# Score products of two attention branches: contraction over 128 rows in place of 64 and 96, on one Trainium2 core

## The chip, the core and the metric

The kernel runs on one core of one Trainium2 chip. The metric is the device time of an execution in microseconds (us); lower is better. Three executions of the kernel before took 1120.05, 1120.86 and 1121.12 us. The engines are named as the profile names them: PE is TensorE (PEld its weight loads), DVE is VectorE, ACT is ScalarE, POOL is GpSimd, SP issues the DMAs.

## The reference

Two decoder layers over 512 tokens of width 1024, in float32. Each layer norms x, multiplies it by one wide input matrix, and feeds four branches; their gated outputs are projected, merged and projected again. Two of the branches compute scores from queries and keys:

```python
# branch A: indexer, top 128 keys of each query, softmax attention over them (4 heads of 64)
idx_logits = jnp.einsum('bqhd,bsd->bqhs', iqb, ik)            # 4 indexer heads of 32, one key of 32
score = jnp.einsum('bqh,bqhs->bqs', iwb * IDX_W_SCALE, relu(idx_logits))
logits = jnp.einsum('bqhd,bqkhd->bhqk', qb, k_sel) * scale
# branch C: stick-breaking attention (4 heads of 64)
z = jnp.einsum('bqhd,bshd->bhqs', qb, k) * scale
wts = jnp.where(strict, jnp.exp(log_sigmoid(z) + after), 0.0)  # after: sums of log(1 - beta) over later keys
```

## The kernel before, in words

Every float32 operand of a product is held as two float32r halves, an upper one (h: the value rounded by a copy on ACT, `half_h`) and a lower one (l: what the rounding left, a subtraction on DVE, `half_l`). A product of two such operands is three matmuls, hh + hl + lh (`mm3`, lines 269 to 271). A head has 64 channels, so half of the 128 partitions would be idle in a score product; the kernel before uses this to save a matmul.

- Branch C, `use_cq` (line 673): the upper half of a head's queries stands twice, on partitions 0 to 63 and 64 to 127 of `cq`; the lower half stands once, in `cql[c]`, where the two heads of a pair share a tile (one on each half of the partitions). `use_ck` (line 682) puts the upper half of the keys on one half of the partitions of `ck` and the lower on the other. In `zmm` (line 699) the first matmul of a key block (line 703) contracts over 128 rows and gives (kh + kl) qh; the second (line 704) contracts over the 64 rows `rs` alone and adds kh ql. The blocks of a head have 512, 384, 256 and 128 columns; the last two share a PSUM bank and are one call, `zmm(2)`.
- Branch A, `use_t1` (line 641): after the rotary step and four transposes (`qktr`) the queries of a tile are kept as upper half and, on the other half of the partitions, lower half (`qT`), the upper half of the keys twice (`kT`), the lower once (`kTl`). `attend` (line 873) computes, for a head and two tiles of queries, a matmul over 128 rows (line 951) and one over 64 (line 952) for each tile, `lg`, with 128 and 256 columns in the first four units of a layer and 384 and 512 in the last four.
- The indexer, `use_t2` (line 795): three pieces of 32 columns, (h, h, l) of the queries against (h, l, h) of the keys, are put beside each other in `ist`, transposed (`iqtr`, `iktr`, lines 822 and 824), and contracted over 96 rows in `select` (line 847, `sc`).

Weights come in chunks of up to [128, 1024] by DMA (`raw`), are split on ACT (`wh`, line 246) and DVE (`wl`, line 248), four steps ahead of their use at most. A step is one group of products on PE. The order on each engine is the order in which the code runs: jobs (generators) hand over at `HOP`, `PE` and `STEP`, and their instructions stand in the engines' queues among the splits of that step. So an instruction of `use_cq` on DVE stands ahead of the weight split that is queued after it. The first layer begins with the jobs of `use_t1` for all four tiles of tokens beside the steps of `cq` and `ck`; then comes `CV` (`tpairs`, the product `tp`, whose two chunks are split during the steps of `ck`).

```python
                    nc.tensor.matmul(o, ck[:, 2 * c + b, ks], cq[:, 2 * c + b, j * P:], start=True, stop=False)
                    nc.tensor.matmul(o, ck[rs, 2 * c + b, ks], cql[c][rs, j * P:], start=False, stop=True)
```

Of the kernel before, what the change touches and what calls it, by code (L numbers as in the profile page):

```python
# [50 lines left out]
# Weight chunks in the order of their use, each [128, 1024] or less.  "t": some tiles of 128 rows with all  # L51
# columns of a group (tokens on the partitions of the product); "c": all rows of 128 columns (columns on the
# partitions); "w": half of the columns of a branch's projection; "p": half of w_ple.
# [11 lines left out]
# groups that take two tiles of tokens through each half of the chunks  # L65
# [7 lines left out]
def chunk_plan():  # L73
    """(kind, elements of a partition, argument, first step, last step) of each chunk of each layer."""
# [50 lines left out]
def lay_weights(w_in, w_branch, w_out, w_ple, w_ple_gate):  # L125
    parts = []

    def rows_in(a):
        """[n * 128, c] to [128, n * c]."""
        return a.reshape(-1, P, a.shape[1]).transpose(1, 0, 2).reshape(P, -1)  # L130
# [22 lines left out]
# buffers of each kind, and how many steps ahead of its use a weight chunk is split  # L153
QB, TB, SB, RAWB, WB, LEAD = 10, 25, 24, 3, 6, 4
# steps from the end of their operands to the stick-breaking heads, the selection and the attention, and the
# rounds of the selection in a step of B, D, the gates and the merges
STICKD, SELECT0, ATTEND0, RATES = 3, 8, 5, (1, 2, 3, 2)
# the start: sums of squares, norm, transposes, evacuation of a tile of tokens, split of the next weight chunk
# and products (of a tile of tokens with a chunk)
# [5 lines left out]
def split_steps(chunks):  # L165
    """The step in which each chunk is split in halves, and whether after the step's products."""
# [14 lines left out]
def hybrid_kernel(ctx: ExitStack, tc: tile.TileContext, w, x, p_t, pos, inv_freq, rows, small, ws_t, b_sp, out):  # L181
# [18 lines left out]
    def halves_cm(name):  # L200
        """Two split tiles of channels: (h, l), each [128, 2, 512]."""
        q = Q(name)
        return q[:, 0:2], q[:, 2:4]

    def halves_tm(name):
        """256 split columns of each tile of tokens: (h, l), each [128, 4, 256]."""
        q = Q(name).rearrange("p (a k) (b f) -> p a (k b) f", a=2, b=2)
        return q[:, 0], q[:, 1]

    def stacked(name):  # L210
        """256 columns of each tile of tokens, each head's 64 as their halves: [128, 4, 4, (h, l), 64]."""
        return Q(name).rearrange("p t (n a f) -> p t n a f", n=4, a=2)
# [38 lines left out]
    def due(late):  # L251
        """The splits of this step."""
# [13 lines left out]
    def mm3(ps, a, b, start, stop):  # L266
        """ps += a.T b of two split operands."""
# [25 lines left out]
    # A job yields HOP where another engine goes on, PE before products that wait for what it has just told,  # L293
    # and STEP behind them.
# [3 lines left out]
    def rounds(live):  # L298
        """Goes round the jobs until each of them has ended or waits; those that wait for products."""
# [47 lines left out]
    def row(l, o, name):  # L347
        """1024 of rows, on every partition."""
# [31 lines left out]
    # key blocks of a unit, with the column at which each starts  # L380
# [37 lines left out]
    def make_masks():  # L418
# [4 lines left out]
        # -1 where row >= column  # L423
# [4 lines left out]
        # far below where the key (row) is not before the query (column)  # L428
# [6 lines left out]
    def rstd(v, parts, n):  # L435
        """v = (sum(parts) / n + eps) ** -0.5 of columns."""
# [8 lines left out]
    def rstd2(v, ss):  # L445
        """The same of two halves of which the first is divided and has eps."""
# [4 lines left out]
    def turn_blocks(name, src):  # L451
        """The four [128, 128] blocks of src, each transposed."""
# [23 lines left out]
    def weigh(out, v, j, n, wh, wl, start, stop):  # L476
        """The keys of block j by their weights: the halves of the values' products, one above the other."""
# [13 lines left out]
    def tgroup(lhs, cols, use, apart=None, finish=None):  # L491
        """Token-major products: use(t, psum) is the job that goes on with a tile of tokens.  With apart,
        two tiles at a time, the second job that many steps behind the first.  With finish, the
        last tile goes by halves of the columns: finish(t, psum, columns) is their job."""
# [24 lines left out]
    def tpairs(lhs, use):  # L519
        """The same for 256 columns, two tiles at a time."""  # L520
# [11 lines left out]
    def ccol(use):  # L532
        """Channel-major products of the normed input: use(psum) is the job that goes on."""
        k, = take()
        ps = bank("cc")
        step(lambda: cmm(ps, k))
        front.append(use(ps))
# [45 lines left out]
    # the first group of products takes tokens and weights as they come in  # L583
# [27 lines left out]
    for l in range(L):  # L611
# [12 lines left out]
        kT = Q("kT")  # L624
        kTl = halves_cm("kTl")[0]
# [15 lines left out]
        def use_t1(t, ps):  # L641
# [5 lines left out]
            # queries: the upper half and, on the other half of the partitions, the lower; keys: the upper  # L647
            # half twice, and the lower
# [3 lines left out]
            k = kT.rearrange("p (c b) s -> p c b s", c=2)  # L652
# [5 lines left out]
            for b in range(2):  # L658
                half_l(q[ROWS[b], :, b], q[ROWS[1 - b], :, b], pv[ROWS[b], 0:2], QK_SCALE)
                half_l(k[ROWS[b], :, b, sl], kTl[ROWS[b], :, sl], pv[ROWS[b], 2:4])  # L660
# [8 lines left out]
        chained[0] = False  # L669
        cq, ck = Q("cq"), Q("ck")  # L670
        cql = [T(f"cql{c}", dt=F32R) for c in range(2)]

        def use_cq(c, ps):
            """Queries of two heads: the upper half twice (on both halves of the partitions), and the lower."""
# [4 lines left out]
            for b in range(2):  # L679
                half_l(cq[ROWS[b], 2 * c + b], cql[c][ROWS[b]], ps[ROWS[b]], QK_SCALE)  # L680

        def use_ck(c, ps):
            """Keys of two heads: the upper half and, on the other half of the partitions, the lower."""
# [11 lines left out]
        def stick(c, b):  # L695
# [3 lines left out]
            def zmm(u):  # L699
                ps = bank("cz")  # L700
                for j, c0 in UNITS[u]:
                    o, ks = ps[:, c0:c0 + S - j * P], slice(j * P, (j + 1) * P)
                    nc.tensor.matmul(o, ck[:, 2 * c + b, ks], cq[:, 2 * c + b, j * P:], start=True, stop=False)
                    nc.tensor.matmul(o, ck[rs, 2 * c + b, ks], cql[c][rs, j * P:], start=False, stop=True)
                return ps

            def smm(u):
                """Sums over the keys behind each key, without those of the later blocks in common()."""
# [5 lines left out]
            def sums(ps, first, blocks, own=None):  # L714
                """Sums of blocks of keys; of their own, over the later keys."""
# [6 lines left out]
            def common():  # L722
                """What the two last blocks of keys add to both of the first."""
# [71 lines left out]
        def use_t2(t, ps):  # L795
# [8 lines left out]
            # query halves (h, h, l) against key halves (h, l, h), stacked along the contraction  # L804
            st = T("ist", (P, 5, 3, 32), F32R)
            rq = r[:, :128].rearrange("p (h f) -> p h f", h=4)
            rk = r[:, 128:160]
            if t:
                A.copy(st[:, 0:4, 0], rq)
                A.copy(st[:, 0:4, 1], rq)  # L810
            A.copy(st[:, 4, 0], rk)
            A.copy(st[:, 4, 2], rk)
            yield HOP
            if t:
                V.tensor_tensor(st[:, 0:4, 2], rq, st[:, 0:4, 0].bitcast(F32), op=ALU.subtract)
            V.tensor_tensor(st[:, 4, 1], rk, st[:, 4, 0].bitcast(F32), op=ALU.subtract)
            yield PE
            sf = st.rearrange("p h c f -> p h (c f)").bitcast(F32)
            if t:
                tp = bank("iqtr")  # L820
                for h in range(4):
                    nc.tensor.transpose(tp[:96, h * P:(h + 1) * P], sf[:, h], ident)
            tk = bank("iktr")
            nc.tensor.transpose(tk[:96, :P], sf[:, 4], ident)
            yield STEP
            if t:
                q = T("iqT", dt=F32R)
                A.copy(q[:96], tp[:96])
                iqT[t] = q
            V.tensor_copy(ikT[:96, t * P:(t + 1) * P], tk[:96, :P])  # L830
# [5 lines left out]
        def select():  # L836
            """bias[i]: 0 at the keys that each query of tile i keeps, far below at the others."""
# [460 lines left out]
```

## Time and profile before

| what | value |
|---|---|
| executions | 1120.05, 1120.86, 1121.12 us (median 1120.86) |
| span of the profiled execution | 1118.6 us, first to last instruction |
| median less span | 2.3 us, what lies around the span |
| PE busy | 1109.1 us (99%), 5300 matmuls |
| DVE busy | 760.5 us (68%) |
| ACT busy | 492.6 us (44%) |
| POOL busy | 23.7 us (2%) |
| chain that ended last | PE 95% |
| granted TensorE clock | mean 1.000 |

The profile's busy time of PE counts overlapped, pipelined matmuls, so 99% does not say that PE works at its peak; the distance between the starts of two matmuls that follow each other does. In a timeline row the columns are start (us), duration (us), engine, line, operation, output and inputs, shape (rows of contraction * columns of the stationary operand, then the moving operand), count, and, in brackets, idle time of the engine before it with what ended it.

### The profile page before, as it was taken

How to read it: one execution, taken by the hardware profiler on the slowest of the kernel's cores; microseconds unless marked ns; L12 is line 12 of the kernel's file. 1: busy time of each engine (PE TensorE's matmuls, PEld its weight loads, DVE VectorE, ACT ScalarE, POOL GpSimd, SP SyncE). 2: the span in 40 equal slices, each digit the busy share in tenths (PEclk: the TensorE clock that was granted, in tenths of full speed). 3: DMA queues.
4: the chain of work that ended last, by engine and by line, in shares of the span. 5: the costliest groups of instructions: out<-in, count | busy, mean ns of one | idle time of the engine just before them, and what ended most of it. 6: DMA issues, size and time to landing. Idle time of an engine off the chain costs nothing.

```text
span 1118.6 us, 13984 instructions
## 1 busy us (share of the span) xinstructions
PE 1109.1 (99%) x5300; PEld 924.3 (83%) x5300; DVE 760.5 (68%) x1420; ACT 492.6 (44%) x857; POOL 23.7 (2%) x46
## 2 busy tenths in 40 slices
PE   8999999999999999999999999999999999999998
PEld 6888888888888888888788988988888888888887
DVE  5967769866788754547577677698668886454562
ACT  5566654323423433434446576433243244333341
POOL 2000000000000000000000000000000000000000
PEclk9999999999999999999999999999999999999999
DMA  5232232322233223542522222313222322226331
GB/s 193 84 109 76 76 99 58 113 76 76 76 94 94 76 90 99 170 151 95 166 97 81 78 74 76 100 61 111 82 86 71 99 76 76 95 94 205 114 114 38
DMA packets 34349, 109.01 MB, mean 97 GB/s; under 512 B 4057, under 2 KB 4841, under 8 KB 34282
## 3 DMA queue, kind: packets, MB, share of 16 engines
q1 hardware_dynamic: 34218, 108.10, 30.2%
q8 instruction: 41, 0.67, 0.2%
q0 software_dynamic: 64, 0.03, 0.1%
q14 instruction: 26, 0.21, 0.1%
HBM read 103.91 MB, written 4.19 MB: 97 GB/s over the span
## 4 chain that ended last, share of the span: by engine, by line
PE 95%; ACT 1%; DVE 1%; DMA 1%; issue 1%; SPq 0%; POOL 0%; DVEq 0%; ACTq 0%
PE mg L269 11%; PE mg L270 10%; PE mg L271 10%; PE tg L269 7%; PE tg L271 7%; PE tg L270 7%; PE cc L269 6%; PE cc L271 6%; PE cc L270 6%; PE z L270 3%; PE z L271 3%; PE z L269 3%; PE tp L270 1%; PE tp L269 1%; PE cs L719 1%; PE tp L271 1%
## 5 line engine op out<-in xcount | busy, mean ns | idle before, releaser
L248 DVE TENSOR_TENSOR wl<-raw,wh 128x1024 fp32r<-128x1024 f32 (+1 forms) x180 | 217.2, 1211 | 19.6 <-ACT wh L246 18.8
L269 PE MATMUL mg<-hh,wh 128*128 128x512 f32 x512 | 201.0, 392 | 0.0
L270 PE MATMUL mg<-hl,wh 128*128 128x512 f32 x512 | 199.4, 389 | 0.0
L271 PE MATMUL mg<-hh,wl 128*128 128x512 f32 x512 | 199.3, 389 | 0.0
L246 ACT CAST wh<-raw 128x1024 fp32r<-128x1024 f32 (+1 forms) x180 | 185.4, 1038 | 10.6 <-DMA raw<-in_w 4.1
L1085 ACT ACTIVATE g<-mg,prm 128x512 f32<-128x512 f32 x64 | 44.2, 690 | 231.0 <-PE mg L271 231.0
L269 PE MATMUL cc<-hh,wh 128*128 128x512 f32 x320 | 126.0, 394 | 0.0
L271 PE MATMUL cc<-hh,wl 128*128 128x512 f32 x320 | 124.8, 390 | 0.0
L270 PE MATMUL cc<-hl,wh 128*128 128x512 f32 x320 | 124.7, 390 | 0.0
L269 PEld LDWEIGHTS mg<-hh,wh 128*128 128x128 f32 x512 | 96.1, 188 | 21.9 <-issue 1.5
L271 PEld LDWEIGHTS mg<-hh,wl 128*128 128x128 f32 x512 | 96.1, 188 | 20.1
L270 PEld LDWEIGHTS mg<-hl,wh 128*128 128x128 f32 x512 | 96.1, 188 | 19.4
L1091 DVE SCALAR_TENSOR_TENSOR g<-g,z 128x512 f32<-128x512 f32 x48 | 32.9, 686 | 72.7 <-PE z L271 72.6
L271 PEld LDWEIGHTS cc<-hh,wl 128*128 128x128 f32 x320 | 60.1, 188 | 12.8
L269 PEld LDWEIGHTS cc<-hh,wh 128*128 128x128 f32 x320 | 60.1, 188 | 12.3 <-issue 0.7
L270 PEld LDWEIGHTS cc<-hl,wh 128*128 128x128 f32 x320 | 60.2, 188 | 11.6
L865 DVE MAX8 m<-cur 128x8 f32<-128x256 f32 (+2 forms) x96 | 53.6, 559 | 4.4 <-POOL cur L857 2.6
L866 DVE MATCH_REPLACE8 cur<-m,cur 128x256 f32<-128x256 f32 (+2 forms) x96 | 52.1, 543 | 0.0
L269 PE MATMUL tg<-wh,xh 128*128 128x512 f32 (+1 forms) x136 | 51.7, 380 | 0.0
L271 PE MATMUL tg<-wh,xl 128*128 128x512 f32 (+1 forms) x136 | 51.3, 377 | 0.0
L270 PE MATMUL tg<-wl,xh 128*128 128x512 f32 (+1 forms) x136 | 51.3, 377 | 0.0
L269 PE MATMUL tg<-wh,mh 128*128 128x512 f32 x128 | 50.0, 390 | 0.0
(251 smaller groups left out, 2019.5 us busy)
## 6 DMA issues: line engine op xcount, KB each, us to landing
raw<-in_w SPq DMA_DIRECT2D x172, 512.0 KB, 3.5
raw<-in_w SPq DMA_DIRECT2D x8, 420.0 KB, 3.1
x<-in_x SPq DMA_DIRECT2D x8, 256.0 KB, 5.6
res<-in_x SPq DMA_DIRECT2D x8, 256.0 KB, 4.3
xdram<-res SPq DMA_DIRECT2D x8, 256.0 KB, 3.5
res<-xdram SPq DMA_DIRECT2D x8, 256.0 KB, 5.6
out<-res SPq DMA_DIRECT2D x7, 256.0 KB, 2.1
gpost<-in_rows SPq DMA_DIRECT2D x2, 512.0 KB, 5.7
```

The costliest lines, as they stand in the source:

```text
L246: A.copy(h[:, :n], r[:, :n])
L248: V.tensor_tensor(lo[:, :n], r[:, :n], h[:, :n].bitcast(F32), op=ALU.subtract)
L269: nc.tensor.matmul(ps, ah, bh, start=start, stop=False)
L270: nc.tensor.matmul(ps, ah, bl, start=False, stop=False)
L271: nc.tensor.matmul(ps, al, bh, start=False, stop=stop)
L719: nc.tensor.matmul(ps[:, (i - first) * P:], tri if i == own else ones, sh[u][q][:, ci:ci + S - i * P], start=(i == blocks[0] and q == 0), ...
L865: V.max(m8, cur[:, :n])
L866: V.match_replace(cur[:, :n], m8, cur[:, :n], TAKEN)
L1085: A.activation(g, ps, AF.Tanh, bias=b_merge(n, dt), scale=0.5)
L1091: V.scalar_tensor_tensor(g, g, 1.0, z, op0=ALU.add, op1=ALU.mult)
```

## The change

All score products contract over 128 rows.

- `kTl` becomes a tile of the shape of `kT`: the lower half of the keys stands on both halves of the partitions. `use_t1` writes it twice (a second subtraction for each b). Line 952 multiplies all 128 rows of `qT` (upper and lower half) by it: kl (qh + ql).
- `cql` becomes four tiles, one for each head, with the lower half of the queries on both halves of the partitions; `use_cq` writes each twice. Line 704 multiplies all 128 rows of `ck`: (kh + kl) ql.
- The indexer stacks four pieces of 32, (h, h, l, l) against (h, l, h, l), in two tiles `isq` and `isk` of their own in place of `ist`; transposes, copies and products take 128 rows.

```diff
-        kTl = halves_cm("kTl")[0]
+        kTl = Q("kTl")
...
-                half_l(k[ROWS[b], :, b, sl], kTl[ROWS[b], :, sl], pv[ROWS[b], 2:4])
+                for o in (ROWS[b], ROWS[1 - b]):
+                    half_l(k[o, :, b, sl], kl[o, :, b, sl], pv[ROWS[b], 2:4])
...
-        cql = [T(f"cql{c}", dt=F32R) for c in range(2)]
+        cql = [T(f"cql{h}", dt=F32R) for h in range(4)]
...
-                half_l(cq[ROWS[b], 2 * c + b], cql[c][ROWS[b]], ps[ROWS[b]], QK_SCALE)
+                for o in (ROWS[b], ROWS[1 - b]):
+                    half_l(cq[o, 2 * c + b], cql[2 * c + b][o], ps[ROWS[b]], QK_SCALE)
...
-                    nc.tensor.matmul(o, ck[rs, 2 * c + b, ks], cql[c][rs, j * P:], start=False, stop=True)
+                    nc.tensor.matmul(o, ck[:, 2 * c + b, ks], cql[2 * c + b][:, j * P:], start=False, stop=True)
...
-            st = T("ist", (P, 5, 3, 32), F32R)
-            rq = r[:, :128].rearrange("p (h f) -> p h f", h=4)
+            sk = T("isk")[:, :P].rearrange("p (a b f) -> p a b f", a=2, b=2)
             rk = r[:, 128:160]
+            rk2 = rk[:, None, :].to_broadcast([P, 2, 32])
             if t:
-                A.copy(st[:, 0:4, 0], rq)
-                A.copy(st[:, 0:4, 1], rq)
-            A.copy(st[:, 4, 0], rk)
-            A.copy(st[:, 4, 2], rk)
+                sq = T("isq", (P, 4, 2, 2, 32))
+                rq = r[:, :128].rearrange("p (h f) -> p h f", h=4)
+                for a in range(2):
+                    A.copy(sq[:, :, 0, a].bitcast(F32R), rq)
+            for a in range(2):
+                A.copy(sk[:, a, 0].bitcast(F32R), rk)
             yield HOP
             if t:
-                V.tensor_tensor(st[:, 0:4, 2], rq, st[:, 0:4, 0].bitcast(F32), op=ALU.subtract)
-            V.tensor_tensor(st[:, 4, 1], rk, st[:, 4, 0].bitcast(F32), op=ALU.subtract)
+                for a in range(2):
+                    V.tensor_tensor(sq[:, :, 1, a], rq, sq[:, :, 0, a], op=ALU.subtract)
+            V.tensor_tensor(sk[:, :, 1], rk2, sk[:, :, 0], op=ALU.subtract)
...
-                            nc.tensor.matmul(ps[k][:, :n], iqT[i][:96, (h + k) * P:(h + k + 1) * P], ikT[:96, :n], start=True, stop=True)
+                            nc.tensor.matmul(ps[k][:, :n], iqT[i][:, (h + k) * P:(h + k + 1) * P], ikT[:, :n], start=True, stop=True)
...
-                        nc.tensor.matmul(ps[:, :w], qT[t][rs, c, n % 2], kTl[rs, c, :w], start=False, stop=True)
+                        nc.tensor.matmul(ps[:, :w], qT[t][:, c, n % 2], kTl[:, n, :w], start=False, stop=True)
```

The number and the order of the instructions on PE, ACT, POOL and SP stay as they are. On DVE, 30 instructions are added. The first place is DVE's queue in the first layer, from the last job of `use_t1` to the splits of the two chunks of `CV` (the `wl` rows). Before:

```order
L285 SCALAR_TENSOR_TENSOR qT<-qktr,qT 64x2x128
L283 TENSOR_TENSOR kTl<-qktr,kT 64x2x128
L285 SCALAR_TENSOR_TENSOR cql_438<-cc,cq 64x512 x2
L248 TENSOR_TENSOR wl_593<-raw_431,wh_592 128x1024
L283 TENSOR_TENSOR ck<-cc,ck 64x512 x2
L248 TENSOR_TENSOR wl_636<-raw_456,wh_635 128x1024
```

And in the change:

```order
L285 SCALAR_TENSOR_TENSOR qT<-qktr,qT 64x2x128
L283 TENSOR_TENSOR kTl<-qktr,kT 64x2x128 x2
L285 SCALAR_TENSOR_TENSOR cql_439<-cc,cq 64x512 x2
L285 SCALAR_TENSOR_TENSOR cql_440<-cc,cq 64x512 x2
L248 TENSOR_TENSOR wl_601<-raw_431,wh_600 128x1024
L283 TENSOR_TENSOR ck<-cc,ck 64x512 x2
L248 TENSOR_TENSOR wl_650<-raw_458,wh_649 128x1024
```

A second `kTl` subtraction stands behind each first one (eight in a layer), and two more of `cql` behind each pair (four in a layer); the splits `wl` come after them, in the same order as before.

The second place is DVE's queue during the stick-breaking heads of the first layer, at a tile of the indexer. Before:

```order
L248 TENSOR_TENSOR wl_1007<-raw_827,wh_1006 128x1024
L815 TENSOR_TENSOR ist<-ir,ist 128x4x32
L816 TENSOR_TENSOR ist<-ir,ist 128x32
L283 TENSOR_TENSOR cwl<-cz,cwh 128x384
L740 SCALAR_TENSOR_TENSOR csp<-cz,csp 128x384
```

And in the change (whose lines stand two to five further down):

```order
L248 TENSOR_TENSOR wl_1021<-raw_841,wh_1020 128x1024
L820 TENSOR_TENSOR isq<-ir,isq 128x4x32 x2
L821 TENSOR_TENSOR isk<-ir,isk 128x2x32
L283 TENSOR_TENSOR cwl<-cz,cwh 128x384
L742 SCALAR_TENSOR_TENSOR csp<-cz,csp 128x384
```

One subtraction more stands ahead of the stick-breaking head's `cwl`, for three of the four tiles of a layer.

## Rows read from the trace of the kernel before

**Rows 1.** The page, busy time and share of each engine.
```profile
PE 1109.1 (99%) x5300; PEld 924.3 (83%) x5300; DVE 760.5 (68%) x1420; ACT 492.6 (44%) x857; POOL 23.7 (2%) x46
```
**Rows 2.** Groups of PE by shape: line, count | busy us, mean ns | idle before.
```profile
L704 PE MATMUL cz<-cql,ck 64*128 64x384 f32 x8 | 3.5, 439 | 0.0
L847 PE MATMUL sc<-ikT,iqT 96*128 96x384 f32 x8 | 2.1, 338 | 0.0
L480 PE MATMUL cav<-cwl,vc 128*128 128x384 f32 x8 | 2.7, 335 | 0.0
```
**Rows 3.** Timeline of PE, 131.0 to 133.0 us, branch C in the first layer.
```profile
131.09 0.28 PE L703 MATMUL cz<-cq,ck 128*128 128x256 f32 x1
131.30 0.38 PE L704 MATMUL cz<-cql,ck 64*128 64x256 f32 x1
131.61 0.33 PE L703 MATMUL cz<-cq,ck 128*128 128x128 f32 x1
131.87 0.32 PE L704 MATMUL cz<-cql,ck 64*128 64x128 f32 x1
132.12 0.39 PE L479 MATMUL cav<-cwh,vc 128*128 128x256 f32 x1
132.35 0.28 PE L480 MATMUL cav<-cwl,vc 128*128 128x256 f32 x1
132.47 0.22 PE L479 MATMUL cav<-cwh,vc 128*128 128x128 f32 x1
132.53 0.28 PE L480 MATMUL cav<-cwl,vc 128*128 128x128 f32 x1
132.64 0.44 PE L719 MATMUL cs<-sph,tri 128*128 128x512 f32 x1
132.92 0.39 PE L719 MATMUL cs<-spl,tri 128*128 128x512 f32 x1
```
**Rows 4.** Timeline of PE, 382.4 to 384.6 us, a late unit of the attention.
```profile
382.45 0.42 PE L951 MATMUL lg<-kT,qT 128*128 128x384 f32 x1
382.81 0.44 PE L952 MATMUL lg<-kTl,qT 64*128 64x384 f32 x1
383.18 0.50 PE L951 MATMUL lg<-kT,qT 128*128 128x512 f32 x1
383.61 0.50 PE L952 MATMUL lg<-kTl,qT 64*128 64x512 f32 x1
384.04 0.50 PE L269 MATMUL mg<-hh,wh 128*128 128x512 f32 x1
384.38 0.39 PE L270 MATMUL mg<-hl,wh 128*128 128x512 f32 x1
```
**Rows 5.** Groups by shape, DVE: the lower half of the keys.
```profile
L283 DVE TENSOR_TENSOR kTl<-qktr,kT 64x256 fp32r<-64x256 f32 x16 | 6.8, 422 | 0.2
```
**Rows 6.** Timeline of DVE, 55 to 64 us, first layer.
```profile
55.99 0.42 DVE L285 SCALAR_TENSOR_TENSOR qT<-qktr,qT 64x256 fp32r<-64x256 f32 x1 [0.34 <-ACT kT L277]
...
58.42 1.39 DVE L285 SCALAR_TENSOR_TENSOR cql<-cc,cq 64x512 fp32r<-64x512 f32 x2 [0.70 <-ACT cq L279]
59.84 1.23 DVE L248 TENSOR_TENSOR wl<-raw,wh 128x1024 fp32r<-128x1024 f32 x1
...
62.52 1.23 DVE L248 TENSOR_TENSOR wl<-raw,wh 128x1024 fp32r<-128x1024 f32 x1
```
**Rows 7.** Timeline of PE, 61 to 66 us, first step of `CV`.
```profile
63.80 0.39 PE L270 MATMUL tp<-wl,hh 128*128 128x256 f32 x1 [0.27 <-DVE wl L248]
```
**Rows 8.** Timeline of DVE, 607 to 610 us, second layer: the same split.
```profile
608.42 1.22 DVE L248 TENSOR_TENSOR wl<-raw,wh 128x1024 fp32r<-128x1024 f32 x1
```
**Rows 9.** Timeline of PE, 614 to 615.2 us: the matmul that needs that split.
```profile
614.75 0.28 PE L270 MATMUL tp<-wl,hh 128*128 128x256 f32 x1
```
**Rows 10.** Waits: engine and line, waited for, total us, times, longest us.
```profile
DVE pr L902 <- PE lg L952: 37.2, 28, 3.5
...
DVE qT L285 <- ACT kT L277: 7.1, 4, 5.1
```

More of the change, by code (lines that the diff above doesn't have):

```diff
@@ L651, in use_t1 @@
             sl = slice(t * P, (t + 1) * P)
-            k = kT.rearrange("p (c b) s -> p c b s", c=2)
+            k, kl = kT.rearrange("p (c b) s -> p c b s", c=2), kTl.rearrange("p (c b) s -> p c b s", c=2)
             for b in range(2):
@@ L803, in use_t2 @@
             half_l(va[:, t, :, 0], va[:, t, :, 1], heads(ps[:, 0:256]))
-            st = T("ist", (P, 5, 3, 32), F32R)
-            rq = r[:, :128].rearrange("p (h f) -> p h f", h=4)
+            sk = T("isk")[:, :P].rearrange("p (a b f) -> p a b f", a=2, b=2)
             rk = r[:, 128:160]
+            rk2 = rk[:, None, :].to_broadcast([P, 2, 32])
             if t:
-                A.copy(st[:, 0:4, 0], rq)
-                A.copy(st[:, 0:4, 1], rq)
-            A.copy(st[:, 4, 0], rk)
-            A.copy(st[:, 4, 2], rk)
+                sq = T("isq", (P, 4, 2, 2, 32))
[4 more added lines that the diff above has]
+                A.copy(sk[:, a, 0].bitcast(F32R), rk)
             yield HOP
             if t:
-                V.tensor_tensor(st[:, 0:4, 2], rq, st[:, 0:4, 0].bitcast(F32), op=ALU.subtract)
-            V.tensor_tensor(st[:, 4, 1], rk, st[:, 4, 0].bitcast(F32), op=ALU.subtract)
+                for a in range(2):
+                    V.tensor_tensor(sq[:, :, 1, a], rq, sq[:, :, 0, a], op=ALU.subtract)
+            V.tensor_tensor(sk[:, :, 1], rk2, sk[:, :, 0], op=ALU.subtract)
             yield PE
-            sf = st.rearrange("p h c f -> p h (c f)").bitcast(F32)
             if t:
@@ L821, in use_t2 @@
                 for h in range(4):
-                    nc.tensor.transpose(tp[:96, h * P:(h + 1) * P], sf[:, h], ident)
+                    nc.tensor.transpose(tp[:, h * P:(h + 1) * P], sq[:, h].rearrange("p a b f -> p (a b f)"), ident)
             tk = bank("iktr")
-            nc.tensor.transpose(tk[:96, :P], sf[:, 4], ident)
+            nc.tensor.transpose(tk[:, :P], sk.rearrange("p a b f -> p (a b f)"), ident)
             yield STEP
@@ L827, in use_t2 @@
                 q = T("iqT", dt=F32R)
-                A.copy(q[:96], tp[:96])
+                A.copy(q, tp)
                 iqT[t] = q
-            V.tensor_copy(ikT[:96, t * P:(t + 1) * P], tk[:96, :P])
+            V.tensor_copy(ikT[:, t * P:(t + 1) * P], tk[:, :P])
         tgroup(hlhs, 420, use_t2, 1)
@@ L944, in attend @@
                     m2, n = units[k]
-                    c, rs = n // 2, slice(64 * (n % 2), 64 * (n % 2) + 64)
+                    c = n // 2
                     lg[k] = []
```

## The prediction

> **What bounds the kernel now.** I read the busy times first, then the groups by shape, then the timelines of PE and DVE around the edited lines, then the waits. PE is busy for 99% of the span [rows 1] and has almost nothing to wait for, so an edit pays only if the matmuls themselves follow each other faster, and costs only where it makes PE wait. Whether they follow fast is read from the distance between two starts. In the stick-breaking head at 131 us [rows 3] the reader finds both patterns side by side, with the same widths. Matmuls over 128 rows: 256 columns take 0.12 us from start to start (132.35 to 132.47), 128 columns 0.06 and 0.11, 512 columns 0.23 or, right behind a 128-column one, 0.28. With the 64-row matmul of line 704 between them: the 256-column matmul of line 703 ahead takes 0.21, the 64-row one 0.31, and the first one behind the block (132.12) still 0.23 where 0.12 is normal. So a 64-row matmul alone costs 0.09 + 0.19 + 0.11 = 0.39 us more than a 128-row one: 0.09 ahead of it, 0.19 itself, 0.11 behind. The attention shows the same [rows 4].
>
> Is it the number of rows? The groups by shape say so: at 384 columns a 64-row matmul lasts 439 ns, the indexer's 96-row one 338, a 128-row one 335 [rows 2]. So 96 rows cost nothing extra, and 64 do.
>
> **What the change removes.** There are 64 such matmuls: in each layer 16 of line 704 and 16 of line 952.
> - The call `zmm(2)` has two of them, with 256 and 128 columns, 8 calls in all. From 131.09 to the second start behind it, 132.35, it takes 1.26 us [rows 3]. At 128 rows the same five distances are 0.12 + 0.12 + 0.06 + 0.11 + 0.17 (0.12, and 0.05 more behind a 128-column matmul) = 0.58. Gain 0.68, times 8: 5.4 us.
> - The calls with 384 and with 512 columns have one each, 16 in all: 0.39 each, 6.2 us.
> - The first four units of the attention in a layer have two, with 128 and 256 columns, 8 in all. I take the 0.68 of `zmm(2)`, less 0.03 because these stand behind 128-column transposes, which make a start late in either kernel: 0.65, 5.2 us.
> - The last four units have 384 and 512 columns, 8 in all. From 382.45 to 384.38 is 1.93 us [rows 4]; at 128 rows 0.18 + 0.18 + 3 x 0.23 = 1.05, and I leave 0.08 for the transposes ahead: gain 0.8, 6.4 us.
>
> Sum: 5.4 + 6.2 + 5.2 + 6.4 = 23.2 us. The indexer's products and transposes go from 96 to 128 rows or columns and gain nothing [rows 2].
>
> The rows say that a 64-row matmul is dearer than a 128-row one, 439 against 335 ns [rows 2]. The Trainium skill, "TensorE: Matmul & The Clock Gate", section "Why this matters for your kernels", states the contrary: one matmul over 32 rows takes as long as one over 128, and few rows pay only where several run at once. By that rule the 23.2 us would be 0 and only the additions below would be left, 1126.3 us (rival 4); the rows contradict it for this kernel, and I go by them.
>
> The gain stays if DVE and ACT keep up with a PE that reaches each point earlier. In the attention they do: DVE waits for the scores in 28 places, 37.2 us in all [rows 10], more than the 11.6 us that the attention saves; with the scores earlier, it starts earlier. In the stick-breaking heads no row shows PE waiting.
>
> **What it adds.** All of it is on DVE.
> - First layer. DVE gets 8 more subtractions of `kTl` and 4 more of `cql` ahead of the splits of `CV`. A `kTl` one lasts 422 ns [rows 5], 0.43 from start to start; two of `cql` take from 58.42 to 59.84 [rows 6], 0.71 each. That is 8 x 0.43 + 4 x 0.71 = 6.2 us. DVE has no room there: the only idle times are 0.34 and 0.70 us, both waits for ACT that the later DVE would no longer see [rows 6], so 5.2 us remain. And the stretch already ends on PE's path: the second split of `CV` runs from 62.52 to 63.75 [rows 6], and the matmul that needs it starts at 63.80, after PE stood idle for it [rows 7]. Nothing covers the shift. This matmul should start at 63.8 + 5.2 = 69.0: **5.2 us lost**, in two waits, a long one at the first split of the group and about 1.2 us at the second. What is queued behind on DVE (keys of `ck`, the split of the next group) is late as well, but its users on PE come later by the same amount.
> - Second layer. The same additions, but the split ends at 608.42 + 1.22 = 609.64 [rows 8] and is needed at 614.75 [rows 9], 5.1 us of cover. The idle times before `qT` come to 7.1 us in four places; 5.1 of it is the wait before the first, 0.3 belongs to the first layer [rows 6, 10], so 1.7 absorb part of the 6.2. A delay of 4.5 us stays under 5.1: cost nothing. Were the cover gone, each us of further delay would be a us of PE.
> - Indexer. Six more subtractions of half the width of a `kTl` one, so at most 6 x 0.42 = 2.5 us if PE waited for all of them; at least 0. PE waits for nothing near them, so I am near the lower end: 0.2 us. Copies of 128 partitions for 96 keep their columns; I take 0.
>
> The upper and lower end of the additions are 7.7 us (6.2, plus 2.5, less the idle 1.0) and, should the second copies cost less than the first or the wait at `CV` be overrated, 0.
>
> **Sum.** The profiled execution spans 1118.6 us; the median of the runs is 1120.9, 2.3 more, and I take these 2.3 as lying outside the span. 1120.9 - 23.2 + 5.2 + 0.2 = **1103.1 us**.
>
> **Rivals.**
> 1. *The stall at `CV` does not come, or is far shorter*: 1120.9 - 23.2 + 0.2 = 1097.9. For it: the idle times of DVE there are few but the shift is a sum of twelve small prices. Against it: PE already waits at exactly this split [rows 7].
> 2. *The stall puts TensorE's clock down.* The mean granted clock before is 1.000, the upper level of 2.4 GHz, with PE busy for 99% of the span [rows 1]. After a stall of about 4 us it could be granted 1.2 GHz for a time. The step of `CV` where this happens has 48 matmuls of 0.12 us [rows 3], 5.8 us; at half the clock all of it would cost 5.8 more, none of it 0. Half: 3 us, 1106. The Trainium skill, "TensorE: Matmul & The Clock Gate", section "Why this matters for your kernels", warns of idle gaps between bursts for this reason; no row of this trace shows a fall.
> 3. *The heads' chains on DVE and ACT become the bound.* PE issues each head's products up to 0.7 us earlier per step, while additions, exponentials and splits between two products take as long as ever. If half of the 11.6 us of the stick-breaking heads is lost in waits for `spl` and `cwl`: 1109. Against it: no such wait shows now; for it: the trace shows no spare time directly either.
> 4. *The number of rows costs nothing, and the change does not do what it is built for* (the other side). Place: the same 64 matmuls. The distances would come from something that stays, such as two matmuls with different moving tiles into one bank. Then the gain is 0 and the stall remains: 1120.9 + 5.4 = 1126.3. It decides as soon as less than 5.4 of the 23.2 us is won, that is, if a second matmul over 128 rows still costs 0.30 of its 0.39 us. Against it: lines 479 and 480 also accumulate two matmuls with different tiles into one bank, at 0.12 and 0.06 [rows 3].
>
> **Chances.** My forecast 0.60; rival 1 0.12; rival 2 0.13; rival 3 0.09; rival 4 0.06. The range 1097.5 to 1108 holds the forecast with its unknown prices and rivals 1 and 2, and leaves out rivals 3 and 4, 0.15. A difference of 0.2% (2.2 us) is about what a measurement can tell from none. All but rival 4 are faster by more; 0.01 of that one I count as no change: faster 0.94, same 0.01, slower 0.05.
>
> **What the profile of the changed kernel would show.** Start-to-start distances of 0.12 and 0.06 us in `zmm(2)`, and groups of lines for the second score product at the same mean as line 480's. PE waiting for `wl` at the `CV` group of the first layer, some 4 us and then 1 us, with DVE without idle time from 47 us to there; no such wait in the second layer. The granted clock at 1.000; below that, rival 2. New waits of PE for `spl`, `cwl` or `isq` would speak for rival 3; distances of 0.3 us at 128 rows for rival 4. The forecast is wrong if the time is above 1108 or below 1097.5, and its working is wrong if the two terms, 23.2 won and 5.2 lost, don't show apart.

## The result, and the profile after

The change takes the kernel from 1120.95 us (median of 4 executions, 1120.05 to 1121.12) to **1103.86 us** (4 executions, 1102.33 to 1104.97): ratio 0.985, 95% interval 0.984 to 0.986. The profiled execution is the one of 1104.97 us; its span is 1103.3.

The busy times of the page after the change, to be read against [rows 1]: PE has 20.6 us less, DVE 11.3 us and 30 instructions more.

```profile
PE 1088.5 (99%) x5300; PEld 923.3 (84%) x5300; DVE 771.8 (70%) x1450; ACT 492.3 (45%) x857; POOL 23.0 (2%) x46
```

Groups of PE by shape after the change, with 384 columns: the second score products of both branches and the indexer's, now all of 128 rows. The 439 ns of [rows 2] are gone; the indexer's 338 ns have become 335.

```profile
L706 PE MATMUL cz<-cql,ck 128*128 128x384 f32 x8 | 2.7, 337 | 0.0
...
L956 PE MATMUL lg<-kTl,qT 128*128 128x384 f32 x8 | 2.7, 335 | 0.0
...
L851 PE MATMUL sc<-ikT,iqT 128*128 128x384 f32 x8 | 2.0, 335 | 0.0
```

Timeline of PE after the change, the same `zmm(2)` as in [rows 3]. From the first start to the second start behind the block it takes 134.97 - 134.39 = 0.58 us, where it took 1.26.

```profile
134.39 0.28 PE L705 MATMUL cz<-cq,ck 128*128 128x256 f32 x1
134.50 0.28 PE L706 MATMUL cz<-cql,ck 128*128 128x256 f32 x1
134.62 0.22 PE L705 MATMUL cz<-cq,ck 128*128 128x128 f32 x1
134.68 0.28 PE L706 MATMUL cz<-cql,ck 128*128 128x128 f32 x1
134.80 0.33 PE L479 MATMUL cav<-cwh,vc 128*128 128x256 f32 x1
134.97 0.28 PE L480 MATMUL cav<-cwl,vc 128*128 128x256 f32 x1
```

The same view, the late unit of the attention of [rows 4]: 380.29 - 379.16 = 1.13 us, before 1.93.

```profile
379.16 0.42 PE L955 MATMUL lg<-kT,qT 128*128 128x384 f32 x1
379.42 0.33 PE L956 MATMUL lg<-kTl,qT 128*128 128x384 f32 x1
379.59 0.39 PE L955 MATMUL lg<-kT,qT 128*128 128x512 f32 x1
379.82 0.40 PE L956 MATMUL lg<-kTl,qT 128*128 128x512 f32 x1
380.06 0.40 PE L269 MATMUL mg<-hh,wh 128*128 128x512 f32 x1
380.29 0.39 PE L270 MATMUL mg<-hl,wh 128*128 128x512 f32 x1
```

That is the gain. The loss stands in the waits of PE after the change (engine, line, waited for: us in total, times, longest). The first row is the wait at `CV` in the first layer; there is no such wait in the second layer, and none for `spl`, `cwl` or `isq`.

```profile
PE tp L270 <- DVE wl L248: 3.8, 1, 3.8
PE htr L455 <- DVE h L566: 2.8, 2, 2.6
PE gpre L359 <- DMA line<-in_rows: 2.4, 1, 2.4
PE htr L455 <- DVE h L1252: 1.1, 1, 1.1
PE tg L269 <- ACT hh L277: 0.5, 1, 0.5
```

The timeline of DVE after the change shows what PE waits for. From 45 us until behind these rows DVE has no idle time; behind the four subtractions of `cql` come the two splits of `CV`, which end at 67.45 and 70.14 (62.52 + 1.23 = 63.75 for the second in [rows 6]).

```profile
63.53 2.79 DVE L285 SCALAR_TENSOR_TENSOR cql<-cc,cq 64x512 fp32r<-64x512 f32 x4
66.24 1.21 DVE L248 TENSOR_TENSOR wl<-raw,wh 128x1024 fp32r<-128x1024 f32 x1
67.48 1.39 DVE L283 TENSOR_TENSOR ck<-cc,ck 64x512 fp32r<-64x512 f32 x2
68.91 1.23 DVE L248 TENSOR_TENSOR wl<-raw,wh 128x1024 fp32r<-128x1024 f32 x1
```

The timeline of PE over the same step. The matmul that needs the first split starts at 67.51 after 3.78 us of idle time, the one that needs the second at 70.23 (63.80 in [rows 7]). Between them the matmuls of 256 columns start 0.21 us apart, and from 73.07 on 0.12.

```profile
63.45 0.28 PE L269 MATMUL tp<-wh,hh 128*128 128x256 f32 x1
67.51 0.58 PE L270 MATMUL tp<-wl,hh 128*128 128x256 f32 x1 [3.78 <-DVE wl L248]
67.89 0.41 PE L271 MATMUL tp<-wh,hl 128*128 128x256 f32 x1
68.10 0.41 PE L269 MATMUL tp<-wh,hh 128*128 128x256 f32 x1
...
70.02 0.41 PE L269 MATMUL tp<-wh,hh 128*128 128x256 f32 x1
70.23 0.54 PE L270 MATMUL tp<-wl,hh 128*128 128x256 f32 x1
...
72.91 0.32 PE L270 MATMUL tp<-wl,hh 128*128 128x256 f32 x1
73.07 0.28 PE L271 MATMUL tp<-wh,hl 128*128 128x256 f32 x1
73.19 0.28 PE L269 MATMUL tp<-wh,hh 128*128 128x256 f32 x1
...
75.70 0.28 PE L705 MATMUL cz<-cq,ck 128*128 128x256 f32 x1
```

Why 0.21: the stretches of 3 us, in the same execution (stretch, its length, busy time of PE, PEld, DVE, ACT and POOL with their instructions, granted TensorE clock, DMA share, GB/s). PE did nearly nothing from 63.7 to 67.5; the clock was still granted in full until about 66 and was at half, 1.2 for 2.4 GHz, from there to 73.

```profile
63.00:66.00 3.00, 0.73 (x4) 0.38 (x2) 2.93 (x6) 2.31 (x5) 0.00 (x0) 1.00 0.00 0
66.00:69.00 3.00, 1.49 (x7) 1.49 (x8) 2.92 (x5) 1.04 (x1) 0.00 (x0) 0.53 0.15 30
69.00:72.00 3.00, 3.00 (x15) 2.96 (x15) 2.92 (x4) 0.00 (x0) 0.00 (x0) 0.50 0.55 189
72.00:75.00 3.00, 3.00 (x24) 3.00 (x23) 0.62 (x1) 0.00 (x0) 0.00 (x0) 0.83 0.62 180
75.00:78.00 3.00, 3.00 (x28) 3.00 (x27) 1.61 (x4) 2.07 (x5) 0.00 (x0) 1.00 0.08 30
```

From the first matmul of `CV` to the head's first product the step lasts 75.70 - 63.45 = 12.25 us; before it was 68.10 - 61.81 = 6.29. So it costs 5.96 us. 4.8 of them had passed at 70.23, when the second split was there, and at either clock that matmul could have started 0.1 us earlier at most, since the split ended at 70.14. The other 1.2 come behind it, where matmuls still ran at half the clock: from there to the head 5.47 us against 4.30. This is one execution; two runs below have the same wait and lose less behind it.

### The profile page after: what moved, and what is told of

Read it like the earlier page. It is cut to its first block, busy times and chain, and to the rows that moved or that the text cites. A ratio compares the mean times of both kernels' runs of the same rounds, so it can differ in the third digit from the quotient of the medians.

```text
span 1103.3 us, 14018 instructions
## 1 busy us (share of the span) xinstructions
PE 1088.5 (99%) x5300; PEld 923.3 (84%) x5300; DVE 771.8 (70%) x1450; ACT 492.3 (45%) x857; POOL 23.0 (2%) x46
## 4 chain that ended last, share of the span: by engine, by line
PE 93%; DVE 4%; DMA 1%; issue 1%; ACT 1%; SPq 0%; POOL 0%; DVEq 0%; ACTq 0%
PE mg L269 11%; PE mg L271 11%; PE mg L270 11%; PE tg L269 7%; PE tg L271 7%; PE tg L270 7%; PE cc L269 6%; PE cc L270 6%; PE cc L271 6%; PE z L270 3%; PE z L269 3%; PE z L271 3%; PE tp L270 2%; PE tp L271 1%; PE tp L269 1%; PE cs L721 1%
```

## Experiments

Theory: the gain comes from the 64 products alone (some 23 us); the loss from twelve subtractions on DVE ahead of the two splits of `CV` (5 to 6 us with the clock's part); the indexer does nothing. The rivals stand in the expectations. In the runs of the first four, the kernel before has a median of 1120.92 us (9 executions), in those of the last four 1121.14 us (15).

### The cost alone

```diff
-                    nc.tensor.matmul(o, ck[:, 2 * c + b, ks], cql[2 * c + b][:, j * P:], start=False, stop=True)
+                    nc.tensor.matmul(o, ck[rs, 2 * c + b, ks], cql[2 * c + b][rs, j * P:], start=False, stop=True)
...
-                        nc.tensor.matmul(ps[:, :w], qT[t][:, c, n % 2], kTl[:, n, :w], start=False, stop=True)
+                        nc.tensor.matmul(ps[:, :w], qT[t][rs, c, n % 2], kTl[rs, n, :w], start=False, stop=True)
```

> The cost alone: all second copies of the lower halves are made as in the change (kTl and cql on both halves of the partitions, the indexer over 128 rows), but the second score products of the attention and of the stick-breaking heads still contract over 64 rows. Theory (the twelve subtractions ahead of the splits of CV stall PE there and the stall puts the clock down for a time; nothing else of the additions costs): the time of the kernel before, 1121.0, plus 5 to 6.5 us, so 1126 to 1127.5; PE waits some 4 us for wl at the first CV group in the first layer, the granted clock falls there, and the products of 64 rows lie 0.31 us from their successors as before. Rival A (the stall costs nothing, or something else of the additions pays for it): 1121 within 0.5. Rival B (the gain came from another order or from the indexer, not from the rows of these 64 products): near 1104.

Measured: 1126.50 us (1125.52 to 1127.69, 5 executions), ratio 1.005 (1.004 to 1.007): 5.6 us slower, in the range of the theory and outside both rivals. The timeline of PE has the same wait:

```profile
65.38 0.40 PE L270 MATMUL tp<-wl,hh 128*128 128x256 f32 x1 [3.79 <-DVE wl L248]
```

Behind it the matmuls start 0.21 us apart again. The change without its gain costs what the forecast set against the gain. In the profiled execution the step of `CV` lasts 11.47 us, 5.2 more than before: 4.8 up to the matmul that needs the second split, as in the change, but only 0.4 behind it. The clock fell about 0.2 us after PE had started again (mean 0.81 from 65 to 66 us, 0.50 from 66 to 69), and from 69.07 on the starts are 0.12 apart. Another 0.5 us arise at the `htr` between the layers.

### The gain alone

```diff
-                for o in (ROWS[b], ROWS[1 - b]):
-                    half_l(k[o, :, b, sl], kl[o, :, b, sl], pv[ROWS[b], 2:4])
+                half_l(k[ROWS[b], :, b, sl], kl[ROWS[b], :, b, sl], pv[ROWS[b], 2:4])
+            for _ in range(6):
+                yield STEP
+            for b in range(2):
+                V.tensor_copy(kl[ROWS[1 - b], :, b, sl], kl[ROWS[b], :, b, sl])
...
-                for o in (ROWS[b], ROWS[1 - b]):
-                    half_l(cq[o, 2 * c + b], cql[2 * c + b][o], ps[ROWS[b]], QK_SCALE)
+                half_l(cq[ROWS[b], 2 * c + b], cql[2 * c + b][ROWS[b]], ps[ROWS[b]], QK_SCALE)
+            for b in range(2):
+                for _ in range(3):
+                    yield STEP
+                V.tensor_copy(cql[2 * c + b][ROWS[1 - b]], cql[2 * c + b][ROWS[b]])
```

> The gain alone: the change, but the second copy of each kTl and cql is made later, by a copy on DVE from the first one, queued behind the splits of CV. All products, their rows and their order on PE are those of the change, and DVE has the same number of additional instructions. Theory: without the stall the change gives its whole gain, 1121.0 - 23.5 = 1097.5 (1096.5 to 1098.5), with a wait of 0.5 us at most at CV in the first layer and a mean granted clock of 1.000. Rival A (the chains of the heads on DVE and ACT, or DVE's work as such, cost the 5 to 6 us, and the wait at CV only shows it first): it stays within 2 us of 1103.9, with waits in another place. Rival B (the stall cost less than the distance of the two starts says): 1100 to 1102.

Measured: 1100.23 us (1099.27 to 1101.15, 4 executions), ratio 0.982 (0.980 to 0.983): faster than the change by 3.6, yet 2.7 us short of the theory. The stall at `CV` is gone (0.3 us of wait as before, clock in full), but rival A is right in part: PE has new waits in the stick-breaking heads and at the indexer. The time lies in the range of rival B, whose condition fails: the step of `CV` is back to 6.31 us, 5.9 less than in the change.

```profile
85.38 0.50 PE L727 MATMUL cs<-sph,tri 128*128 128x512 f32 x1 [0.38 <-ACT sph L277]
86.10 0.50 PE L727 MATMUL cs<-spl,tri 128*128 128x512 f32 x1 [0.22 <-DVE spl L283]
...
92.03 0.33 PE L834 MATMUL iktr<-ident,isk 128*128 128x128 f32 x1 [0.48 <-DVE isk L827]
```

Start by start against the change, six places lose time: 0.5 us at 85.4, 0.6 at 86.1, 1.0 at 92.0, 0.4 at 98.6 and, in the second layer, 0.1 at 633.0 and 0.3 at 638.5, together 2.9 us, about what is missing. The copies of `kTl` had moved to 79.7 to 88 us, into DVE's queue ahead of `spl` and `isk`. The first two places, 1.1 us, come before DVE's first instruction of the indexer (88.17). DVE's shortage does not end at `CV`.

### The attention alone, the heads alone

Of the change only the edits of `kTl` and line 952, and only those of `cql` and line 704:

```diff
-                        nc.tensor.matmul(ps[:, :w], qT[t][rs, c, n % 2], kTl[rs, c, :w], start=False, stop=True)
+                        nc.tensor.matmul(ps[:, :w], qT[t][:, c, n % 2], kTl[:, n, :w], start=False, stop=True)
```

> One part alone: only the attention's second product goes to 128 rows (kTl on both halves); cql and the indexer stay as before. Theory: gain 5.2 + 6.4 = 11.6 us, up to 12.0 with the matmuls behind the blocks; on DVE eight subtractions of 0.43 = 3.4 us ahead of the splits of CV, less 1.0 idle = 2.4 us of stall; sum 1121.0 - 11.8 + 2.4 = 1111.6 if the clock stays at 1.000 through the shorter stall, some 1 us more if it falls. Rival (the attention gains nothing because DVE's work on the weights sets its pace): 1123.4.

```diff
-                    nc.tensor.matmul(o, ck[rs, 2 * c + b, ks], cql[c][rs, j * P:], start=False, stop=True)
+                    nc.tensor.matmul(o, ck[:, 2 * c + b, ks], cql[2 * c + b][:, j * P:], start=False, stop=True)
```

> The other part alone: only the second product of the stick-breaking heads goes to 128 rows (cql on both halves); kTl and the indexer stay as before. Theory: gain 5.4 + 6.2 = 11.6 us, up to 12.0 with the matmuls behind the blocks; four subtractions of 0.71 = 2.8 us ahead of the splits of CV, less 1.0 idle = 1.8 us of stall; sum 1121.0 - 11.8 + 1.8 = 1111.0 with the clock at 1.000. Rival (the heads' chains on DVE and ACT become the bound and give half of it back): 1117, with new waits of PE for spl or cwl.

Measured: the attention alone 1111.47 us (1110.60 to 1111.78, 4 executions), ratio 0.992 (0.990 to 0.993); the heads alone 1110.57 us (1110.21 to 1111.14, 4), ratio 0.991 (0.990 to 0.992). Theory 1111.6 and 1111.0: both hold, both rivals fall. In the attention alone PE waits twice at `CV`, as the forecast had it for the change, and the matmuls behind either wait start 0.12 us apart:

```profile
63.73 0.39 PE L270 MATMUL tp<-wl,hh 128*128 128x256 f32 x1 [1.43 <-DVE wl L248]
63.95 0.28 PE L271 MATMUL tp<-wh,hl 128*128 128x256 f32 x1
64.07 0.29 PE L269 MATMUL tp<-wh,hh 128*128 128x256 f32 x1
...
66.41 0.39 PE L270 MATMUL tp<-wl,hh 128*128 128x256 f32 x1 [0.98 <-DVE wl L248]
```

The two parts alone win 9.45 + 10.35 = 19.8 us, together only 17.1. In the profiled executions the step of `CV` loses 2.4 and 1.5 us alone (forecast 2.4 and 1.8) and 6.0 together, 2.1 more. Of these, 1.0 is by the working DVE's idle time, which each part alone uses for itself, and 1.2 the half clock, which only the long wait of both brings; some 0.6 of the 2.7 us is left, within what three such differences are uncertain by.

### Is it the rows, or the change of rows?

The kernel before, with the four products of a unit in another order:

```diff
-                    lg[k] = []
-                    for i in range(2):
-                        t = 2 * m2 + i
-                        w = (t + 1) * P
-                        ps = bank("lg")
-                        nc.tensor.matmul(ps[:, :w], qT[t][:, c, n % 2], kT[:, n, :w], start=True, stop=False)
-                        nc.tensor.matmul(ps[:, :w], qT[t][rs, c, n % 2], kTl[rs, c, :w], start=False, stop=True)
-                        lg[k].append(ps)
+                    lg[k] = [bank("lg") for _ in range(2)]
+                    for lo in range(2):
+                        for i, ps in enumerate(lg[k]):
+                            t = 2 * m2 + i
+                            w = (t + 1) * P
+                            if lo:
+                                nc.tensor.matmul(ps[:, :w], qT[t][rs, c, n % 2], kTl[rs, c, :w], start=False, stop=True)
+                            else:
+                                nc.tensor.matmul(ps[:, :w], qT[t][:, c, n % 2], kT[:, n, :w], start=True, stop=False)
```

> What makes a product of 64 rows dear: itself, or standing beside one of 128 rows. The kernel before, with the four score products of an attention unit in another order: the two of 128 rows first, then the two of 64 rows, which now stand beside each other (same operands, sizes and sums; one change from 128 to 64 rows and one back in a unit in place of two). 16 units in all. Theory A (changing between 64 and 128 rows costs 0.39 us each time there and back, however many products of 64 rows stand between): 16 x 0.39 = 6.2 us faster, 1114.7, and the two products of 64 rows start as far apart as two of 128 rows (0.06 for 128 columns, 0.18 for 384). Theory B (0.20 of it comes with the change, the 0.19 belong to each product of 64 rows): 16 x 0.2 = 3.2 us faster, 1117.7. Theory C (each product of 64 rows costs its 0.39 wherever it stands): 1121.0.

Measured: 1115.74 us (1114.87 to 1117.44, 5 executions), ratio 0.995 (0.994 to 0.996): 5.4 us faster with the same 64-row products. The late unit of [rows 4] in this order (its two products of 128 rows and its two of 64 stand in one row each):

```profile
382.62 0.66 PE L954 MATMUL lg<-kT,qT 128*128 128x384 f32 x2
383.20 0.67 PE L952 MATMUL lg<-kTl,qT 64*128 64x384 f32 x2
383.81 0.50 PE L269 MATMUL mg<-hh,wh 128*128 128x512 f32 x1
384.15 0.40 PE L270 MATMUL mg<-hl,wh 128*128 128x512 f32 x1
```

From 382.62 to 384.15 is 1.53 us. With four changes of rows it was 1.93, with none it is 1.13: 0.40 us for two changes, 0.80 for four, so **0.20 us for each change** in a late unit, and nothing is left for the 64 rows themselves. An early unit takes 1.45, 1.16 and 0.77 us: 0.15 to 0.19 for each change, and by the same account up to 0.05 for each product of 64 rows. In the starts one by one it is 0.1 in the gap ahead of the change and 0.1 in the next. One sign that theory A named did not come: its two products of 64 rows start 0.28 us apart with 384 columns and 0.16 with 128, not 0.18 and 0.06. That is the 0.1 in the gap behind the change. The new order also moves to another bank between two products; the change keeps the old order and has no excess, so the bank is not the cause.

The weight loads (PEld) of the second products show more: the first one before, the second one of 64 rows in the grouped order, and the first one after the change.

```profile
382.81 0.18 PEld L952 LDWEIGHTS lg<-kTl,qT 64*128 64x128 f32 x1 [0.19 <-issue]
...
383.31 0.19 PEld L952 LDWEIGHTS lg<-kTl,qT 64*128 64x128 f32 x1
...
379.25 0.19 PEld L956 LDWEIGHTS lg<-kTl,qT 128*128 128x128 f32 x1
```

At a change the load starts only with its product (both at 382.81 [rows 4]). Without a change it starts some 0.17 us ahead, under the product before it: at 379.25 for the product at 379.42, and at 383.31 for the one at 383.49, between the two products of 64 rows. That this is what the change costs is likely, but no run tests it alone.

On time, this is theory A; theory B's 1117.7 and theory C's 1121.0 lie outside the interval. Its sum of 6.2 was a little high, since an early unit has an excess of 0.68 and not 0.78 us: 8 x 0.29 + 8 x 0.40 = 5.5.

The Trainium skill, "TensorEngine Tiling (Array Packing)", section "Tiling Modes", says that changing the tiling mode drains TensorE, without a price, and lists arrays of 64 rows among the modes. The trace agrees in that each change between 64 and 128 rows costs time, up to 0.20 us; no row shows a drain as such.

### 96 rows in the same place

```diff
-                    nc.tensor.matmul(o, ck[:, 2 * c + b, ks], cql[2 * c + b][:, j * P:], start=False, stop=True)
+                    nc.tensor.matmul(o, ck[:96, 2 * c + b, ks], cql[2 * c + b][:96, j * P:], start=False, stop=True)
...
-                        nc.tensor.matmul(ps[:, :w], qT[t][:, c, n % 2], kTl[:, n, :w], start=False, stop=True)
+                        nc.tensor.matmul(ps[:, :w], qT[t][:96, c, n % 2], kTl[:96, n, :w], start=False, stop=True)
```

> The number of rows by itself, in the same place. The change, but the second product of the attention and of the stick-breaking heads contracts over partitions 0 to 95 in place of all 128, so a third of the terms that the change adds is left out. All else is that of the change. Theory (only 64 rows are dear; 96 rows run as 128 do, as the indexer's products showed): 1103.9 within 1 us and start-to-start distances of 0.12 for 256 columns. Rival (the price follows the unused rows): half of the 23.5 us comes back, 1115.6.

Measured: 1103.63 us (1103.01 to 1105.43, 4 executions), ratio to before 0.984 (0.983 to 0.986); the time of the change, while the rival's is 1115.6. A `zmm(2)` takes 0.58 us as in the change, a late unit 1.16 for 1.13. 32 unused rows cost next to nothing; the price does not follow the unused rows. For time alone the kernel leaves out rows 96 to 127: half of the terms that the change adds (not a third) for one head of each pair, and half of the needed ones for the other.

The step of `CV` has the wait here too (3.74 us). The clock fell 0.7 us after PE had started again: the starts are 0.12 us apart up to 66.46 and 0.21 from there to 69.66, but for the wait at the second split. The step lasts 11.60 us, 5.3 more than before: 4.7 up to the second split and 0.6 behind it.

### The indexer alone

Of the change, only the edits of `ist`, `isq` and `isk` and the slices of `iqT` and `ikT`:

```diff
-                            nc.tensor.matmul(ps[k][:, :n], iqT[i][:96, (h + k) * P:(h + k + 1) * P], ikT[:96, :n], start=True, stop=True)
+                            nc.tensor.matmul(ps[k][:, :n], iqT[i][:, (h + k) * P:(h + k + 1) * P], ikT[:, :n], start=True, stop=True)
```

> The third part of the change alone: the kernel before with the indexer over 128 rows (four pieces, isq and isk) in place of 96. Theory: no gain, and 0 to 0.5 us of cost from the second subtraction in front of the transposes: 1121.0 to 1121.5. Rival (leaving tiles of 96 rows saves something too): 8 products, 32 transposes, at 0.1 us each at most 4 us, 1117.

Measured: 1120.84 us (1119.62 to 1121.29, 10 executions) against 1121.14, ratio 0.9996 (0.9987 to 1.0005). No difference: the expected cost of 0 to 0.5 us does not show, and the rival's 1117 falls.

### The copies later still

Against the run with later copies; the indexer as in the kernel before:

```diff
-            for _ in range(6):
-                yield STEP
-            for b in range(2):
-                V.tensor_copy(kl[ROWS[1 - b], :, b, sl], kl[ROWS[b], :, b, sl])
+        def second():
+            kl = kTl.rearrange("p (c b) s -> p c b s", c=2)
+            for t in range(NT):
+                for b in range(2):
+                    sl = slice(t * P, (t + 1) * P)
+                    V.tensor_copy(kl[ROWS[1 - b], :, b, sl], kl[ROWS[b], :, b, sl])
+                    yield STEP
...
         idle.append(later(select(), SELECT0))
+        idle.append(later(second(), 12))
```

> A version meant to keep the whole gain: attention and stick-breaking heads at 128 rows, the indexer as in the kernel before (96 rows), the second copies of cql made behind the splits of CV as in the run with later copies, those of kTl much later still, one in each step of branch B, ahead of the attention's first use. The run with later copies lost 2.7 us in six new waits of PE between 85 and 105 us and at the indexer of the second layer, where DVE had fallen behind. Theory (these waits came from the eight copies of kTl that still stood ahead of the heads' work on DVE, and from the indexer's additional subtractions): 1097.5 (1096.5 to 1098.5), without waits of PE for sph, spl, isk or isq, the granted clock at 1.000. Rival (the heads' chains on DVE are the bound with the faster products, wherever the copies stand): it stays at 1100.2.

Measured: **1097.73 us** (1097.09 to 1098.07, 4 executions), ratio to before 0.979 (0.978 to 0.980). It is the fastest of all: 23.4 us faster than before, 6.1 faster than the change, in the range of the theory; the rival's 1100.2 is outside. The waits of PE name neither `sph`, `spl`, `isk` nor `isq`, and at `CV` 0.3 us as before:

```profile
...
PE htr L455 <- DVE h L566: 2.1, 2, 1.8
PE htr L455 <- DVE h L1263: 1.0, 1, 1.0
PE tg L269 <- ACT hh L277: 0.9, 1, 0.9
PE tp L270 <- DVE wl L248: 0.3, 1, 0.3
```

The losses of the run with later copies went with the copies of `kTl` and the indexer's second subtractions. The first 1.1 us come from the copies, since they lie ahead of the indexer; which of the two brought how much of the rest was not tried apart.

## Why the prediction was right, point by point

The time was forecast at 1103.1 and measured at 1103.86. Both terms show apart. In the loss, two small errors partly cancel: DVE's delay was 0.4 us less than forecast, and the clock, which was left out, cost 0.4 to 1.2.

- **The gain, 23.2 us: right.** The version that keeps all of it and has no stall wins 23.4. Place by place, `zmm(2)` was forecast at 0.58 and took 0.58, the late unit at 1.93 - 0.8 = 1.13 and took 1.13; an early unit won 0.68 where 0.65 stood. Added over all 48 blocks, from the first start to the second start behind, the profiled pair differs by 23.2 us: 5.3 for `zmm(2)`, 6.2 for the calls of one block, 5.4 for the early and 6.3 for the late units.
- **"A 64-row matmul alone costs 0.39 us more": the sum right, the owner wrong.** The step read 0.09 ahead, 0.19 itself and 0.11 behind, and took the number of rows for the cause. The run with grouped products shows two changes of up to 0.20 each, there and back; two 64-row products side by side pay once. The sum came out by luck in this point: in the kernel before every one of the 64 stood between products of 128 rows.
- **The rule weighed there.** The Trainium skill, "TensorE: Matmul & The Clock Gate", section "Why this matters for your kernels", has one matmul over 32 rows as long as one over 128; no run here has 32 rows. The prediction held the rows of the 64-row products against it. By the grouped products the two need not clash: in a late unit all of the 0.40 us belongs to the two changes. What rival 4 made of the rule (no gain at all) fails all the same, since no stream of this kernel is without the changes.
- **The loss at `CV`, 5.2 us: right in place and cause, a little small.** It was 5.96 in the profiled execution, and 5.2 and 5.3 in those of the cost alone and of 96 rows. By the medians, the cost alone is 5.6 us slower than the kernel before, and the change 6.1 slower than the version without the wait. The working gave DVE's delay; that part measured 4.7 to 4.8 in all three. What was missing is the clock.
- **"The granted clock at 1.000": wrong; rival 2 did happen.** Its condition, a stall of about 4 us, was met (3.78), and the clock went to half. Its price of 3 us was too high: the 12 matmuls between the two splits ran at half speed in time in which PE would otherwise have waited for the second split, so the forecast second wait of 1.2 us shrank to about 0.1 (70.23 to 70.57, where 0.21 is the distance beside it), and only the 1.2 us behind were lost (0.4 and 0.6 in the two other profiled executions with such a wait). With the 6.0 of this execution in place of 5.2 the sum is 1103.9.
- **Second layer hidden, indexer nothing: right.** No wait at `CV` in the second layer, and the indexer alone makes no difference.
- **Rival 3 (DVE's chains become the bound): false for the change, true one step further.** It has no wait for `spl` or `isq`, but as soon as the stall went and the copies stood among the heads, DVE was late there, and 2.9 us were lost. DVE's idle time before the attention's `pr` went from 37.2 us in 28 places [rows 10] to 28.5 in 14, with no wait of PE in return.

The four terms of the profiled pair: +1.6 because PE in this execution came to `CV` that much later (63.45 for 61.81), +6.0 at `CV`, -23.3 from there to the end, +0.3 at the `htr` between the layers; -15.4, against -15.3 of the spans. Of the 1.6, 1.5 have arisen by 12 us, ahead of every edited instruction; other executions of the change are up to 2.6 us shorter.

## What to carry to other kernels

Look for matmuls of another shape of rows strewn among full ones, and read the distance from start to start around them, not their own duration: group them, or fill their rows with terms that do no harm, and pay for each change only once or not at all. What the filling needs on another engine belongs behind the work that TensorE is about to wait for; ask for each such instruction when its result is first used, and queue it there. Before adding work to an engine, look for the split that already ends on TensorE's path, because there DVE's delay was PE's: here 4.8 us of it, and the half clock behind the long wait cost 0.4 to 1.2 us more.

## What the runs showed of the hardware

- Changing between products of 64 and of 128 rows cost 0.20 us each way in units of 384 and 512 columns, and 0.15 to 0.19 in those of 128 and 256. In the former, products of 64 rows cost nothing more by themselves; units with products of 96 rows took 1.16 us for 1.13.
- At such a change the weight load started together with its product; without a change in these units it started 0.03 to 0.23 us ahead of it.
- The granted clock fell to half around a wait of 3.7 to 3.8 us in three profiled executions: in that of the change during the wait, with PE busy again from 67.5 on and the clock at half until 73, in the other two 0.2 and 0.7 us after PE had started again. All 13 executions of these three kernels (the change, the cost alone, 96 rows) have a mean granted clock of 0.996 to 0.998; those of the attention alone (waits of 1.4 and 1.0), the heads alone (1.0 at the longest) and the last version 0.999 or 1.000. The Trainium skill, "TensorE: Matmul & The Clock Gate", section "Why this matters for your kernels", warns of idle gaps between bursts for this; the trace agrees.
- On DVE the second copy of a `cql` from the first one took 0.42 us, the second subtraction from PSUM 0.70 (2.79 for four).
